# Low parts of weights by adding DMAs in place of sums on VectorE and GpSimd

## The chip, the core and the metric

The kernel runs on one core of one Trainium2 chip. The metric is device time in microseconds (us) of one execution. Engines go by their names in the profile: PE (TensorE matmuls) and PEld (its weight loads), DVE (VectorE), ACT (ScalarE), POOL (GpSimd) and SP (SyncE, which here only issues DMAs).

## What is computed

A trunk of two pre-norm residual layers on 1024 tokens of 1024 channels. Cut to its core, the reference is:

```python
for i in range(2):
    mod = silu(c) @ ada_w[i] + ada_b[i]                 # adaLN: 6 vectors of 1024
    sh_m, sc_m, g_m, sh_f, sc_f, g_f = split(mod, 6)
    h = rms_norm(x, norm_mix_g[i]) * (1 + sc_m) + sh_m
    y = conformer_conv(h) if i == 0 else multiscale_pool(h)
    x = x + (1 + g_m) * y
    h = rms_norm(x, norm_ffn_g[i]) * (1 + sc_f) + sh_f
    x = x + (1 + g_f) * ((silu(h @ w_gate[i]) * (h @ w_up[i])) @ w_down[i])   # width 2816
return rms_norm(x, final_g)
```

`conformer_conv` is a product to 2048 channels with a gated linear unit, a causal depthwise convolution of width 31 over the tokens, a layer norm with swish, and a product back to 1024 channels. `multiscale_pool` takes trailing means over 2, 4, 8 and 16 tokens and four small products. Everything is float32.

## The kernel before

**Tiling.** Channels lie on the 128 partitions, tokens along the free dimension. The tokens are two chunks of 512, A and B. A weight tile is 128 x 1024 floats (512 KB): for a product with 1024 input channels it holds eight 128 x 128 blocks.

**Split products.** PE runs in the format float32r. To keep float32 precision, both operands are split into a high part (rounded to float32r) and a low part (the remainder), and each product is three matmuls: high x high, high x low and low x high (`products`, L378). So each weight tile has a buffer of twice its size: `wt[:, 0]` is the high part and `wt[:, 1]` the low part. A tile is used in 24 matmuls of 512 columns.

**Loading a weight** (`load_weight`, L369). SP loads the raw tile into a buffer of the pool `raws` (L147, three buffers: `RAW_BUFS`, L37). ACT copies it to `wt[:, 0]`, which rounds it. Then DVE or POOL writes `wt[:, 1] = raw - wt[:, 0]`; `either` (L139) picks the engine whose planned clock is earlier. The pool `wts` has six buffers (`W_BUFS`, L36). A raw buffer is free again when both readers are done, and the buffers of a pool are used in turn.

**The adaLN vectors** use the same pool `raws`. For layer 0, `ada_columns` (L334) loads tiles of `adan` in pairs and multiplies them on PE. For layer 1 and its later vectors, `ada_task` (L296) loads tiles of `ada` one by one, and DVE forms a dot product in place on each (`ada_dot`, L292); SP issues these loads in the same queue as those of the weights. There are 32 tiles of `adan` and, after the start, 48 of `ada`.

**Order.** The order on PE is written by hand: a list of units, each with the weight tiles that it uses. `run_units` (L509) emits them in turn, and its `ahead` (L516) calls `load_weight` for tiles of later units, so that up to six are loaded or in use. Other work (convolution taps, norms, adaLN, pooling) consists of tasks that `pace` (L169) steps between units. A planner keeps a clock for each engine, with a fixed price for each kind of instruction (`PRICES`), and gives a step to DVE or POOL when that clock is not ahead of PE's. A scheduler then sets the final order of the engines other than PE.

**The convolution's taps** (`Taps`, L579) are 31 steps for each of 16 tiles of 128 x 512. DVE adds a tap in one instruction, into `ca`. On POOL, ACT first forms the product `pr`, and POOL adds it to `pa`. DVE joins the two at the end.

**Course.** The first stage computes the first adaLN vectors and, with eight tiles loaded for it alone, half of the first product for chunk A. Then come the rest of the first product for A and B with the taps of A behind it, the layer norm and output product of A, the feed-forward part of layer 0 for A with the taps of B behind it, the output product of B, the feed-forward part of layer 0 for B with the adaLN vectors of layer 1, and layer 1. A feed-forward unit uses two tiles (gate and up); after each group of three units comes one with three tiles (down).

In the rows below, nearly all instructions of DVE, ACT and POOL have the line L95, and PE's L117, since a helper issues them; L372 is the load of a weight, L127 and L134 are other loads.

Of the kernel before, what the change touches and what calls it, by code (L numbers as in the profile page):

```python
# [9 lines left out]
F32 = mybir.dt.float32  # L10
F32R = mybir.dt.float32r
I32 = mybir.dt.int32
AF = mybir.ActivationFunctionType
ALU = mybir.AluOpType
MUL, ADD, SUB = ALU.mult, ALU.add, ALU.subtract

P = 128
D = 1024
# [82 lines left out]
def trunk(ctx, tc, xT, c, vec, ada, adan, w1, w2, wgu, wdn, wpl, out):  # L101
    nc = tc.nc
    ctx.enter_context(tc.manual_schedule(engines={mybir.EngineType.PE}))
    clock = {"PE": 0.0, "V": 0.0, "G": 0.0, "S": 0.0}
    V_ = Engine(nc.vector, "V", clock, PRICES["V"], lambda i: order(i))
    G_ = Engine(nc.gpsimd, "G", clock, PRICES["G"], lambda i: order(i))
    S_ = Engine(nc.scalar, "S", clock, PRICES["S"], lambda i: order(i))
# [11 lines left out]
    def order(ins):  # L119

        if behind[0] and last_mm[0] is not None:
            tc.add_manual_dep(ins.ins, last_mm[0], edge, reason="behind the products")
        return ins
# [15 lines left out]
    def either(n):  # L139

        now = clock["PE"]
        v, g = (max(clock[e], now) + engines[e].price("tensor_tensor", n) for e in "VG")
        return V_ if v <= g else G_
# [9 lines left out]
    def nm(s):  # L153
        uid[0] += 1
        return f"{s}_{uid[0]}"
# [13 lines left out]
    def pace(ahead=AHEAD):  # L169

        for t in [t for t in tasks if t.urgent or getattr(t, "free", False)]:
            while step(t, "V"):
                pass
        moved = True
        while moved and tasks:
            moved = False
            for e in "VG":
                if clock[e] < clock["PE"] + ahead:
                    moved = any(step(t, e) for t in list(tasks)) or moved
# [186 lines left out]
        return mod[:, b : b + 1]  # L366


    def load_weight(src, n=D, load=nc.sync.dma_start):  # L369
        raw = raws.tile([P, D], F32, tag="raw", name=nm("raw"))[:, :n]  # L370
        dst = raw if len(src.shape) == 2 else raw.rearrange("p (a b) -> p a b", a=src.shape[1])
        load(dst, src)  # L372
        wt = wts.tile([P, 2, D], F32R, tag="w", name=nm("w"))
        S_.copy(wt[:, 0, :n], raw)
        either(n).tensor_tensor(wt[:, 1, :n], raw, wt[:, 0, :n].bitcast(F32), op=SUB)
        return wt

# [131 lines left out]
    def run_units(cap, early):  # L509

        queue = [w for ws, _ in units for w in ws]
        loaded = list(early)
        del queue[: len(early)]
        used = [0]

        def ahead(free):  # L516
            while queue and len(loaded) + used[0] - free < cap:
                loaded.append(load_weight(queue.pop(0)))
                if len(loaded) > 1:
                    break  # L520

        for ws, emit in units:
            def take():
                ahead(0)
                used[0] += 1
                return loaded.pop(0)
            emit(take)
            used[0] -= len(ws)
            ahead(0)
            pace()  # L530
# [379 lines left out]
    for k in range(KT + 1):  # L910
        if k < KT:
            w = wts.tile([P, 2, D], F32, tag="w", name=nm("adaw"))
            load_next(w, ada_m[0, k][:, 0:2, :])
            ada_dot(w[:, 1], 0, 1, k)
            tc.add_manual_dep(V_.last.ins, t_last if k else rstd_last, edge, reason="behind the first norm")
        if k > 0:
            dot = V_.last.ins.name
            V_.scalar_tensor_tensor(h_a[k - 1][1], t, mod[:, k - 1 : k], h_a[k - 1][0].bitcast(F32), op0=ADD, op1=SUB)
            if k < KT:
                tc.add_manual_dep(V_.last.ins, dot, edge, reason="the scalar engine's part takes that long")  # L920
            for q in range(2 * FIRST):
                products(fb[q], wt, q, h_a[k - 1], k == 1, k == KT)
        if k < KT:
            ada_dot(w[:, 0], 0, 0, k)
            V_.tensor_scalar(scale_m[:, k : k + 1], mod[:, KT + k : KT + k + 1], scale_b[:, k : k + 1], V("norm_mix_g", k), op0=ADD, op1=MUL)
            V_.tensor_tensor(mod[:, k : k + 1], mod[:, k : k + 1], V("ada_b", k), op=ADD)
            t = temp(A.n)
            V_.scalar_tensor_tensor(t, x[0][k], scale_m[:, k : k + 1], rstd_a, op0=MUL, op1=MUL)
            t_last = V_.last.ins.name
            S_.activation(h_a[k][0], t, AF.Identity, bias=mod[:, k : k + 1])  # L930
            wt = load_weight(w1k[k], 2 * FIRST * P, load_next)
    for e in clock:
        clock[e] = max(clock.values())
    early = [load_weight(w1[FIRST, i], load=load_next) for i in range(2)]
    for k in range(KT):
        load_next(x[1][k], xT[:, k, B.t0 : B.t0 + B.n])
# [154 lines left out]
```

## Time and profile before

| What | Value |
|---|---|
| Median of 3 runs | 1996.76 us (1985.09 to 1997.44) |
| Time of the profiled execution | 1995.5 us |
| Its span, first to last instruction | 1993.7 us |
| Mean granted TensorE clock | 0.957 of full speed |
| DMA packets and bytes | 71800, 223.91 MB, mean 112 GB/s |

How to read the profile: busy time is the time in which an engine executes; an engine's idle time matters only where PE, or another engine on the chain, waits for it. Matmuls are pipelined, so the mean of one matmul (some 390 ns) is longer than the distance between two. A group row has count, busy time, mean, and the idle time ahead of it with what ended it. DMA issues show the issuing engine's time; the transfer itself is in "us to landing". In the table by stage each row is a stretch of the span. The prediction shows the rows that it uses.

### The profile page before, as it was taken

How to read it: one execution, taken by the hardware profiler on the slowest of the kernel's cores; microseconds unless marked ns; L12 is line 12 of the kernel's file. 1: busy time of each engine (PE TensorE's matmuls, PEld its weight loads, DVE VectorE, ACT ScalarE, POOL GpSimd, SP SyncE). 2: the span in 40 equal slices, each digit the busy share in tenths (PEclk: the TensorE clock that was granted, in tenths of full speed). 3: DMA queues.
4: the chain of work that ended last, by engine and by line, in shares of the span. 5: the costliest groups of instructions: out<-in, count | busy, mean ns of one | idle time of the engine just before them, and what ended most of it. 6: DMA issues, size and time to landing. Idle time of an engine off the chain costs nothing.

```text
span 1993.7 us, 21104 instructions
## 1 busy us (share of the span) xinstructions
PE 1831.9 (92%) x8016; PEld 1483.9 (74%) x8016; DVE 1195.3 (60%) x1554; ACT 711.9 (36%) x979; POOL 772.2 (39%) x533
## 2 busy tenths in 40 slices
PE   6999639788989998689999999999999999999997
PEld 4776417677767886567888888888888888888886
DVE  8889863789984346678846333585563346333334
ACT  3555543555633223223323222342332232222223
POOL 4678942699933213225512111262122221211111
PEclk9999858899999999799999999999999999999998
DMA  8534422122222236374322222323222223222221
GB/s 271 207 107 141 144 84 96 53 85 86 84 85 85 95 124 225 108 251 159 104 98 96 95 95 95 106 81 109 96 96 95 96 95 127 95 96 95 96 94 43
DMA packets 71800, 223.91 MB, mean 112 GB/s; under 512 B 7057, under 2 KB 17425, under 8 KB 71698
## 3 DMA queue, kind: packets, MB, share of 16 engines
q1 hardware_dynamic: 70544, 221.51, 33.2%
q8 instruction: 63, 1.03, 0.2%
q10 hardware_dynamic: 1154, 1.05, 0.2%
q14 instruction: 39, 0.32, 0.1%
HBM read 218.34 MB, written 4.19 MB: 112 GB/s over the span
## 4 chain that ended last, share of the span: by engine, by line
PE 63%; DVE 12%; POOL 10%; issue 6%; DMA 6%; ACT 2%; SPq 0%; DVEq 0%; POOLq 0%; ACTq 0%
PE dn L117 22%; PE gate L117 18%; PE up L117 17%; POOL pa L95 7%; PE y L117 3%; DMA adaw<-in_ada_dram 3%; DVE adaw L95 2%; POOL w L95 2%; DVE acc L95 1%; DVE w L95 1%; DMA raw<-in_w_dram 1%; DVE col L95 1%; DVE t L95 1%; DVE ca L95 1%; DVE x L95 1%
## 5 line engine op out<-in xcount | busy, mean ns | idle before, releaser
L95 POOL TENSOR_TENSOR w<-raw,w 128x1024 fp32r<-128x1024 f32 x148 | 371.0, 2508 | 971.1 <-ACT w L95 952.3
L95 ACT CAST w<-raw 128x1024 fp32r<-128x1024 f32 x312 | 321.2, 1046 | 635.5 <-issue 384.7
L117 PE MATMUL dn<-ghi,w 128*128 128x512 f32 (+1 forms) x1456 | 454.4, 391 | 20.9 <-ACT ghi L95 19.8
L117 PE MATMUL gate<-hhi,w 128*128 128x512 f32 x1408 | 456.1, 393 | 10.4 <-ACT w L95 5.8
L117 PE MATMUL up<-hhi,w 128*128 128x512 f32 x1408 | 454.3, 392 | 0.0
L117 PEld LDWEIGHTS dn<-ghi,w 128*128 128x128 f32 x1456 | 275.8, 192 | 82.3 <-ACT ghi L95 22.3
L117 PEld LDWEIGHTS gate<-hhi,w 128*128 128x128 f32 x1408 | 266.3, 189 | 69.1 <-ACT w L95 6.7
L95 DVE TENSOR_TENSOR t<-t,up 128x512 f32<-128x512 f32 x88 | 60.2, 684 | 412.3 <-PE up L117 405.3
L117 PEld LDWEIGHTS up<-hhi,w 128*128 128x128 f32 x1408 | 266.0, 189 | 55.4
L95 POOL TENSOR_TENSOR pa<-pa,pr 128x512 f32<-128x512 f32 x201 | 286.2, 1445 | 39.0 <-ACT pr L95 34.6
L117 PE MATMUL dn<-glo,w 128*128 128x512 f32 (+1 forms) x728 | 286.0, 393 | 14.4 <-DVE glo L95 9.4
L95 DVE TENSOR_TENSOR w<-raw,w 128x1024 fp32r<-128x1024 f32 x164 | 249.3, 1521 | 56.8 <-ACT w L95 52.8
L95 DVE SCALAR_TENSOR_TENSOR x<-dn,gains,x 128x512 f32<-128x512 f32 (+1 forms) x264 | 190.8, 730 | 154.2 <-PE dn L117 154.0
L117 PE MATMUL gate<-hlo,w 128*128 128x512 f32 x704 | 276.1, 392 | 1.1 <-DVE hlo L95 1.1
L117 PE MATMUL up<-hlo,w 128*128 128x512 f32 x704 | 275.3, 391 | 0.0
L117 PEld LDWEIGHTS dn<-glo,w 128*128 128x128 f32 x728 | 139.4, 191 | 46.1 <-DVE glo L95 11.2
L95 DVE SCALAR_TENSOR_TENSOR ca<-u,vecs,ca 128x512 f32<-128x512 f32 x247 | 172.7, 746 | 0.9
L95 ACT ACTIVATE pr<-u,vecs 128x512 f32<-128x512 f32 x201 | 140.3, 720 | 81.1 <-POOL pa L95 70.6
L117 PEld LDWEIGHTS gate<-hlo,w 128*128 128x128 f32 x704 | 133.4, 189 | 29.4 <-DVE hlo L95 1.6
L117 PEld LDWEIGHTS up<-hlo,w 128*128 128x128 f32 x704 | 133.0, 189 | 27.4
L95 ACT ACTIVATE t<-gate 128x512 f32<-128x512 f32 x88 | 52.5, 597 | 252.9 <-PE gate L117 233.0
L95 DVE SCALAR_TENSOR_TENSOR adaw<-adaw,cact 128x1024 f32<-128x1024 f32 x64 | 86.8, 1358 | 36.0 <-DMA adaw<-in_ada_dram 35.4
(115 smaller groups left out, 1628.1 us busy)
## 6 DMA issues: line engine op xcount, KB each, us to landing
raw<-in_wgu_dram SPq DMA_DIRECT2D x176, 512.0 KB, 3.3
raw<-in_wdn_dram SPq DMA_DIRECT2D x88, 512.0 KB, 3.4
adaw<-in_ada_dram SPq DMA_DIRECT2D x48, 512.0 KB, 4.3
raw<-in_w_dram SPq DMA_DIRECT2D x44, 512.0 KB, 3.5
adan<-in_adan_dram SPq DMA_DIRECT2D x32, 512.0 KB, 4.4
adaw<-in_ada_dram SPq DMA_DIRECT2D x8, 1024.0 KB, 6.7
x<-in_xT_dram SPq DMA_DIRECT2D x16, 256.0 KB, 5.0
raw<-in_wpl_dram SPq DMA_DIRECT2D x4, 512.0 KB, 3.3
```

Of the source, the lines that this page charges most:

```text
L95: self.last = self.order(getattr(self.eng, name)(out, *args, **kw))
L117: last_mm[0] = nc.tensor.matmul(out, lhsT, rhs, start=start, stop=stop).ins.name
```

## The change

`load_weight` gets a parameter `summed`, which `run_units` sets for every tile that it loads; the eight tiles of the first stage and the two that are loaded early call it without. With it, ACT writes a second copy of the raw tile, negated, to `wt[:, 1]`, which rounds to the negated high part. Then a DMA, issued on POOL's queue, adds the raw tile to it in SBUF: raw - high, the low part. The planner's clock of POOL is advanced by 1.0 for it. The raw buffer is free when the DMA has read it. The scratch space for descriptors of such DMAs grows from 256 to 1024 bytes per partition.

```diff
-    def load_weight(src, n=D, load=nc.sync.dma_start):
+    def load_weight(src, n=D, load=nc.sync.dma_start, summed=False):
         raw = raws.tile([P, D], F32, tag="raw", name=nm("raw"))[:, :n]
         dst = raw if len(src.shape) == 2 else raw.rearrange("p (a b) -> p a b", a=src.shape[1])
         load(dst, src)
         wt = wts.tile([P, 2, D], F32R, tag="w", name=nm("w"))
         S_.copy(wt[:, 0, :n], raw)
+        if summed:
+            S_.activation(wt[:, 1, :n], raw, AF.Copy, scale=-1.0)
+            order(nc.gpsimd.dma_start(wt[:, 1, :n].bitcast(F32), raw, accum_op=ADD))
+            clock["G"] = max(clock["G"], clock["PE"]) + 1.0
+            return wt
         either(n).tensor_tensor(wt[:, 1, :n], raw, wt[:, 0, :n].bitcast(F32), op=SUB)
         return wt
...
-                loaded.append(load_weight(queue.pop(0)))
+                loaded.append(load_weight(queue.pop(0), summed=True))
...
-    nc = _bacc.Bacc("TRN2", target_bir_lowering=False, num_devices=1, dynamic_dma_scratch_size=256)
+    nc = _bacc.Bacc("TRN2", target_bir_lowering=False, num_devices=1, dynamic_dma_scratch_size=1024)
```

## The prediction, made before the changed kernel ran

> **What bounds the kernel now.** I read, in this order, the page's busy shares, its chain of work, the busy time by stage, the chain inside the stages that are not full, and the queue of loads on SP.
>
> ```profile
> span 1993.7 us, 21104 instructions
> ...
> PE 1831.9 (92%) x8016; PEld 1483.9 (74%) x8016; DVE 1195.3 (60%) x1554; ACT 711.9 (36%) x979; POOL 772.2 (39%) x533
> ```
> ```profile
> PE 63%; DVE 12%; POOL 10%; issue 6%; DMA 6%; ACT 2%; SPq 0%; DVEq 0%; POOLq 0%; ACTq 0%
> PE dn L117 22%; PE gate L117 18%; PE up L117 17%; POOL pa L95 7%; PE y L117 3%; DMA adaw<-in_ada_dram 3%; DVE adaw L95 2%; POOL w L95 2%; DVE acc L95 1%; DVE w L95 1%; DMA raw<-in_w_dram 1%; DVE col L95 1%; DVE t L95 1%; DVE ca L95 1%; DVE x L95 1%
> ```
>
> PE carries the chain, but not everywhere. The table by stage says where it does not (stretch and its length; busy time and count on PE, weight loads, DVE, ACT, POOL; granted clock; DMA share; GB/s):
>
> ```profile
> 62.00:235.00 173.00, 162.55 (x740) 123.03 (x738) 151.35 (x191) 98.69 (x141) 137.95 (x111) 0.98 0.42 144
> 235.00:305.00 70.00, 21.38 (x75) 9.16 (x75) 45.75 (x77) 31.96 (x51) 38.35 (x30) 0.55 0.30 102
> ...
> 350.00:620.00 270.00, 237.86 (x982) 191.59 (x981) 231.14 (x303) 145.98 (x206) 206.38 (x136) 0.92 0.24 78
> 620.00:715.00 95.00, 95.00 (x419) 78.30 (x418) 32.98 (x37) 24.54 (x30) 19.28 (x8) 1.00 0.28 95
> 715.00:980.00 265.00, 226.23 (x957) 182.86 (x956) 191.08 (x249) 79.73 (x107) 100.54 (x87) 0.92 0.51 170
> 980.00:1960.00 980.00, 980.00 (x4341) 808.73 (x4340) 446.76 (x540) 280.04 (x359) 221.93 (x105) 1.00 0.29 96
> ```
>
> Of the 1994 us, 620 to 715 and 980 to 1960 are PE alone: it is full at clock 1.00, and DVE, ACT and POOL are busy for under half of the time. Nothing taken from them shortens these 1075 us. The rest is in three places: the taps of the first half (to 305), the taps of the second half (350 to 620, DVE 86% and POOL 76% busy), and the adaLN stage (715 to 980), where DMA is at 0.51.
>
> In the full stages one weight tile lasts PE 5.44 us (24 products), which is the rate at which new ones are needed:
>
> ```profile
> 1150.56 5.48 PE gate L117 x24
> 1156.03 5.44 PE up L117 x24
> ```
>
> **What the change does, part by part.** In the built kernels' instruction order, 302 of the 312 weight tiles lose their sum on DVE or POOL and get one ACT instruction (the negated high part) and one DMA issued on POOL's queue that adds the raw tile. The eight tiles of the first stage and two loaded early keep the sum. PE's products are the same. SP's order of loads hardly changes. The planner also moves 26 taps from POOL to DVE (191 steps left on POOL, where there were 217).
>
> The prices of the parts, from the instructions on the tile raw (min/median/max ns) and from the page's DMA parts:
>
> ```profile
> L95 ACT CAST w<-raw x312: 1028/1046/1057, 14.9 to 1943.6; 128x1024 fp32r<-128x1024 f32 x156
> L372 SPq DMA_DIRECT2D raw<-in_wgu_dram x176: 327/328/408, 302.7 to 1912.6; - x176
> L95 DVE TENSOR_TENSOR w<-raw,w x164: 1206/1226/2752, 62.5 to 1939.3; 128x1024 fp32r<-128x1024 f32 x164
> L95 POOL TENSOR_TENSOR w<-raw,w x148: 2338/2393/3963, 16.0 to 1944.7; 128x1024 fp32r<-128x1024 f32 x148
> ```
> ```profile
> q1 hardware_dynamic: 70544, 221.51, 33.2%
> ...
> raw<-in_wgu_dram SPq DMA_DIRECT2D x176, 512.0 KB, 3.3
> ...
> adaw<-in_ada_dram SPq DMA_DIRECT2D x8, 1024.0 KB, 6.7
> ```
>
> *ACT.* 302 x 1.05 = 317 us more, less 26 x 0.7 for taps that leave: about 1010 us, half of the span. In the fullest stretch, 350 to 620, it has 146 of 270 busy and gets some 39 x 1.05 = 41: no bound. Price zero in itself; what covers it is ACT's idle time, and without that each negation would delay the casts and taps queued behind it by 1.05 us.
>
> *The issue on POOL.* No row shows it. Below: an issue on SP, 0.33 us. Above: the sum that it replaces, 2.39 us. I take 1.0, between them and nearer to the issue, as POOL reads no tile for it. The issue waits for the negation, 1.05 us later than the sum did, with POOL's taps queued behind it.
>
> *The adding transfer.* No row shows one either. It reads two tiles of 512 KB and writes one. Below: a load of 512 KB, 3.3 us. Above: a load of 1024 KB, 6.7 us. For the value between: 221.51 MB took 33.2% of 1993.7 us on 16 engines, so 512 KB cost 1.57 us of all engines, and the second read adds that to a landing of 3.4: 5.0 us. In a sentence of its own: the Trainium skill (DMA: Bandwidth & Descriptors, section Anatomy of one DMA) gives a POOL-issued DMA about 2.0 us plus bytes / 436 GB/s, 3.2 us for 512 KB as an estimate, which would make the sum below about 2010 us; no run here shows it yet.
>
> *How long a raw tile is held.* This is the step that decides, because there are three raw buffers for weights and adaLN tiles together, used in turn, with SP's loads in order. Before: load 3.4, cast 1.05, sum 1.23 or 2.39, together 6.2 on average. After: load 3.4, cast and negation 2.1, issue 1.0, transfer 5.0: 11.5. Each weight holds its buffer 5.3 us longer (with the bounds above, 2.9 to 8.4). The sum's place goes to a wait of SP: behind it stand all later loads, and behind those ACT's casts (in order, with the taps' products behind them) and PE.
>
> Where PE is full, three buffers give a tile every 11.5 / 3 = 3.8 us against 5.44, and up to six weight tiles are in hand: hidden, price zero. It would cost if the hold went above 16.3 us, or if the DMA engines became the limit (a rival below).
>
> In the first half, two of the three buffers are held by adaLN tiles that wait for PE, and the weights pass through one. SP's queue (start, length, issues) and the chain there:
>
> ```profile
> 206.94 0.81 SPq L127 DMA_DIRECT2D adan<-in_adan_dram  x2
> 212.39 5.92 SPq L372 DMA_DIRECT2D raw<-in_w_dram  x2
> 219.05 0.80 SPq L127 DMA_DIRECT2D adan<-in_adan_dram  x2
> 224.94 5.90 SPq L372 DMA_DIRECT2D raw<-in_w_dram  x2
> ```
> ```profile
> 210.00 2.38 POOL w L95
> 212.39 3.23 DMA raw<-in_w_dram
> 215.65 1.06 ACT w L95
> 216.73 1.24 DVE w L95
> 217.98 3.38 DMA raw<-in_w_dram
> ```
>
> A load follows straight on the sum that frees its buffer; a pair takes 224.94 - 212.39 = 12.6 us, as much as PE needs for two tiles and its adaLN products. Four such pairs get 2 x 5.3 longer each: 42 us. Most of it is covered, because PE is through with these products early and then waits for the taps:
>
> ```profile
> PEld mean L117 <- DVE acc L95: 37.3, 1, 37.3
> ```
>
> That wait covers 37 us, so 5 are left; for the earlier weights of this half, whose delay starts taps late, I add 10 (an estimate: two weights' 5.3): +15 us.
>
> In the adaLN stage 48 tiles run through the same buffers between weights, and the chain goes from one landing to the dot product that frees the buffer and on to the next load:
>
> ```profile
> 738.60 5.41 DMA adaw<-in_ada_dram
> 744.04 1.24 DVE adaw L95 x2
> 745.30 4.33 DMA adaw<-in_ada_dram
> ```
>
> By the built order of SP, weights stand at nine places among the 48. Each pushes the in-order chain by 5.3: 48 us. I take two thirds, 32 us (an estimate): PE is busy for 226 of the 265 us, so part of the push falls where it has tiles in hand. DMA share is highest here, too, so nothing makes it cheaper.
>
> What the sums' leaving gives, stretch 62 to 305 and 350 to 620 (instructions on the tile w, same columns):
>
> ```profile
> 62.00:305.00 243.00, 146.25 (x621) 116.67 (x619) 25.09 (x17) 26.13 (x25) 21.91 (x9) 0.86 0.38 132
> ...
> 350.00:620.00 270.00, 231.82 (x948) 185.88 (x947) 45.96 (x27) 40.12 (x39) 28.88 (x12) 0.92 0.24 78
> ```
>
> In the second taps stage DVE loses 46 us and POOL 29; POOL gets 39 issues of 1.0 and loses about half of the 26 taps (13 x 1.4 = 18, which cost DVE 13 x 0.75 = 10). POOL, whose taps are on the chain, is left with 39 - 29 - 18 = 8 us less: -8, and DVE's 36 us are mostly not on the path; I take -10. In the first taps stage any gain only shortens that cover and is not counted. At the end (after 1960) no weight is left: zero.
>
> Sum, against the profiled execution's 1995.5 us (span 1993.7 and 1.8 around it; it stands 1.3 below the median of 1996.76): 1995.5 + 15 + 32 - 10 = 2032.5, so **2033 us**. With all lower prices (2.9 us of hold, 0.33 an issue) the terms are 0, 9 x 2.9 x 2/3 = 17 and -25, 1988; with all upper ones (8.4 us, 2.39 an issue, the adaLN push in full) 67 - 37 + 17 = 47, 76 and +30, 2149.
>
> **Rivals.**
>
> *It gets faster: the hold is covered everywhere.* For it: six tiles in hand last PE 33 us, DVE and POOL are nearly full in the taps, and 44 sums of DVE (71 us) and 21 of POOL (51 us) go there against 65 issues: 122 - 65 = 57 us of engine time, half of it on each: -28, so 1967 us. Against it: the chain above steps from sum to load. It decides if a weight is held no more than about 2 us longer, a transfer that lands in 2 us.
>
> *No change.* The lower prices above: gain and loss cancel, about 1995 us.
>
> *The DMA engines become the bound.* Loads take 1.57 us of each 5.44. If the add takes three such shares, 4.7, a tile costs 6.3 and every full stage is 0.84 us per tile longer: 4760 products / 24 = 198 tiles, 167 us, and with the 37 above 2200 us; four shares would give 2510. It decides from 3.9 us of service per add. Against it: two reads are two shares, 3.1 us, together 86% of 5.44. The Trainium skill (Collectives: The Full Stack, section The bandwidth ceiling) says that an adding DMA runs at half of a copy's rate because it reads two sources, not because of the sum; by that rule this rival falls, and no row here shows it.
>
> *The issue costs POOL as much as the sum did.* At 2.4 us, POOL has 65 x 1.4 = 91 us more in the taps than I counted; with half of it on the path, 2079 us. For it: POOL is the slow engine. Against it: in the full stages it would not matter.
>
> **How the numbers follow.** Forecast (slower by holds, 2018 to 2149): 0.47. Issue as dear as the sum: 0.12. DMA engines as the bound: 0.13. No change: 0.11. Faster: 0.17. About 1% is what a measurement of this kernel can tell from none; faster by over 1% is 0.17, within 1% 0.11, slower 0.72. The range runs from 1968, at the rival that ends faster, to 2200, at the DMA rival's mildest case; half of each lies outside, about 0.15 to 0.2. The likeliest case's own range is 2018 to 2149.
>
> **What the changed profile would show.** Right: the full stages unchanged at 5.44 us per tile; SP's loads waiting for the adding DMA, not for DVE or POOL; landings near 5 us; the adaLN stage some 30 us longer; PE's wait for the taps of the first half shorter, as its products end later; fewer PE gaps in 350 to 620. Wrong: landings under 3 us or over 8; a DMA share near 1 and tiles of over 5.5 us in the full stages; POOL idle or busy for over 2 us at each issue; a taps stage that is longer than before.

## The result and the profile after

The changed kernel takes 2012.47 us (median of 4 runs, 2009.98 to 2017.11); the kernel before, measured beside it, 1993.28 us (median of 4, 1985.09 to 1997.44). The ratio is 1.0101, interval 1.0079 to 1.0123: slower by 1%, 19 us. The prediction was 2033 us, slower, with 1968 to 2200 as its range; the range of its likeliest case was 2018 to 2149, and the measured time lies below that. The profiled span goes from 1993.7 to 2008.2 us, 14.5 longer.

The page of the changed kernel, busy shares and the chain that ended last:

```profile
span 2008.2 us, 21898 instructions
...
PE 1841.0 (92%) x8016; PEld 1485.6 (74%) x8016; DVE 912.8 (45%) x1422; ACT 971.9 (48%) x1255; POOL 620.5 (31%) x665
```
```profile
PE 72%; DMA 11%; DVE 7%; ACT 4%; issue 4%; POOL 2%; SPq 0%; DVEq 0%; POOLq 0%; ACTq 0%
```

DVE lost 283 us of work and POOL 152, with the issues of its 302 DMAs (269 us) counted in; ACT, which had room, took 260 more. On the chain DVE and POOL together fell from 22% to 9%, PE rose from 63% to 72%, and DMA from 6% to 11%. So the change does what it says, and the time comes back through the DMAs. What they cost, from the DMA part of the same kernel (queue: packets, MB, share of 16 engines; then KB each and median us to landing):

```profile
q0 software_dynamic: 43488, 158.35, 43.4%
q1 hardware_dynamic: 70544, 221.51, 32.6%
...
w<-raw POOLq DMA_DIRECT2D x302, 512.0 KB, 5.9
raw<-in_wgu_dram SPq DMA_DIRECT2D x176, 512.0 KB, 5.0
```

An add (one adding DMA) lands 5.9 us after its issue began, and a load that runs beside adds takes 5.0 where it took 3.3. An add takes 0.434 x 2008.2 / 302 = 2.89 us of all 16 engines; a load, 512 KB of the 221.51 MB, 1.55. The instructions on the tile raw (min/median/max ns):

```profile
L95 ACT ACTIVATE w<-raw x302: 1046/1054/1064, 71.0 to 1965.5; 128x1024 fp32r<-128x1024 f32 x151
L377 POOL DMA_DIRECT2D w<-raw x302: 832/869/2009, 72.6 to 1966.9; - x151
```

Where the 14.5 us arise is read from two products that stand at the same place in PE's order in both kernels: the output product (y<-vhi; it starts with chunk A behind the first taps and ends with chunk B) and the pooling product (y<-mxhi), whose first matmul follows the adaLN stage. Rows of the tile y, "first start to last start", before and then after:

```profile
L117 PE MATMUL y<-vhi,w x256: 388/389/774, 305.0 to 782.0; 128*128 128x512 f32 x128
...
L117 PE MATMUL y<-mxhi,w x64: 389/389/390, 1022.9 to 1436.2; 128*128 128x512 f32 x64
```
```profile
L117 PE MATMUL y<-vhi,w x256: 388/389/796, 318.0 to 779.0; 128*128 128x512 f32 x128
...
L117 PE MATMUL y<-mxhi,w x64: 389/389/389, 1036.5 to 1449.8; 128*128 128x512 f32 x64
```

That cuts the span into four parts. The first half (to 305.0) is 13.0 us longer, the part with the second taps and output product B (305.0 to 782.0) 16.0 shorter, the adaLN stage (782.0 to 1022.9) 16.6 longer; the rest, up to the last gate product, takes 930.7 us in both. With 0.9 behind that: 13.0 - 16.0 + 16.6 + 0.9 = 14.5. The full stages did not move; a stretch of 50 us in one, with all engines (PE, weight loads, DVE, ACT, POOL, clock, DMA share, GB/s), and the chain in another:

```profile
1500.00:1550.00 50.00, 50.00 (x221) 41.17 (x220) 10.04 (x14) 21.05 (x24) 7.82 (x9) 1.00 0.83 191
```
```profile
1213.37 5.44 PE gate L117 x24
1218.81 5.44 PE up L117 x24
```

PE is busy all the time, 5.44 us a tile, though DMA stands at 0.83 there: 2.89 + 1.55 = 4.44 of each 5.44 us is 0.82.

**The first half after.** SP's queue (start, length, issues), and the chain beside it:

```profile
195.45 11.29 SPq L372 DMA_DIRECT2D raw<-in_w_dram  x4
...
221.15 0.80 SPq L372 DMA_DIRECT2D raw<-in_w_dram  x2
222.04 9.75 SPq L127 DMA_DIRECT2D adan<-in_adan_dram  x2
237.81 0.80 SPq L372 DMA_DIRECT2D raw<-in_w_dram  x2
```
```profile
195.45 3.33 DMA raw<-in_w_dram
...
199.81 1.05 ACT w L95
...
201.26 5.10 DMA w<-raw
...
206.41 5.83 DMA raw<-in_w_dram
...
213.28 1.06 ACT w L95
...
214.74 6.36 DMA w<-raw
...
221.15 3.24 DMA raw<-in_w_dram
```

A load starts some 0.05 us after an add has landed, where it used to follow a sum. Raw tiles are held for 10.9 us (195.45 to 206.36), 14.7 (206.41 to 221.1) and 16.2 (the second load of the pair at 221.15 to 237.76). But the two loads of a pair are issued within 0.80 us (they took 5.92 before): they lie in two buffers side by side, and a pair takes 237.81 - 221.15 = 16.7 us against 12.6.

### The profile page after: what moved, and what is told of

Its sections match the earlier page's. It is cut to its first block, busy times and chain, and to the rows that moved or that the text cites. A ratio compares the mean times of both kernels' runs of the same rounds, so it can differ in the third digit from the quotient of the medians.

```text
span 2008.2 us, 21898 instructions
## 1 busy us (share of the span) xinstructions
PE 1841.0 (92%) x8016; PEld 1485.6 (74%) x8016; DVE 912.8 (45%) x1422; ACT 971.9 (48%) x1255; POOL 620.5 (31%) x665
## 3 DMA queue, kind: packets, MB, share of 16 engines
q0 software_dynamic: 43488, 158.35, 43.4%
q1 hardware_dynamic: 70544, 221.51, 32.6%
## 4 chain that ended last, share of the span: by engine, by line
PE 72%; DMA 11%; DVE 7%; ACT 4%; issue 4%; POOL 2%; SPq 0%; DVEq 0%; POOLq 0%; ACTq 0%
PE dn L117 22%; PE gate L117 21%; PE up L117 20%; DMA w<-raw 4%; PE y L117 3%; DMA adaw<-in_ada_dram 3%; PE first L117 2%; ACT w L95 2%; POOL pa L95 2%; DVE ca L95 2%; DVE acc L95 1%; DVE adaw L95 1%; DMA raw<-in_w_dram 1%; DMA raw<-in_wdn_dram 1%; PE g L117 1%
## 5 line engine op out<-in xcount | busy, mean ns | idle before, releaser
L95 ACT CAST w<-raw 128x1024 fp32r<-128x1024 f32 x312 | 325.3, 1043 | 745.5 <-PE dn L117 244.7
L377 POOL DMA_DIRECT2D w<-raw x302 | 269.1, 893 | 1161.1 <-ACT w L95 1068.8
L117 PE MATMUL dn<-ghi,w 128*128 128x512 f32 (+1 forms) x1456 | 454.7, 391 | 34.7 <-ACT ghi L95 14.8
L95 ACT ACTIVATE w<-raw 128x1024 fp32r<-128x1024 f32 x302 | 318.4, 1054 | 0.0
L95 POOL TENSOR_TENSOR pa<-pa,pr 128x512 f32<-128x512 f32 x175 | 247.5, 1552 | 27.3 <-ACT pr L95 24.4
L95 DVE SCALAR_TENSOR_TENSOR ca<-u,vecs,ca 128x512 f32<-128x512 f32 x273 | 187.9, 747 | 0.9
L95 DVE TENSOR_TENSOR glo<-t,ghi 128x512 fp32r<-128x512 f32 x75 | 55.5, 740 | 237.7 <-ACT ghi L95 237.7
L95 ACT ACTIVATE pr<-u,vecs 128x512 f32<-128x512 f32 x175 | 118.8, 716 | 35.5 <-POOL pa L95 26.2
L95 DVE SCALAR_TENSOR_TENSOR adaw<-adaw,cact 128x1024 f32<-128x1024 f32 x64 | 79.3, 1245 | 55.8 <-DMA adaw<-in_ada_dram 55.6
```

Source lines behind the costliest of these rows:

```text
L95: self.last = self.order(getattr(self.eng, name)(out, *args, **kw))
L117: last_mm[0] = nc.tensor.matmul(out, lhsT, rhs, start=start, stop=stop).ins.name
L377: order(nc.gpsimd.dma_start(wt[:, 1, :n].bitcast(F32), raw, accum_op=ADD))
```

## The experiments

**The theories.** *Holding (H):* the loss comes from raw tiles that are held longer by the negation, the issue and the transfer, while SP's in-order loads wait for one of three buffers. Its rivals: *traffic*, the bytes of the adds that slow the other loads; and *POOL's issue*, with POOL's taps queued behind a DMA that waits for its operand. In the code, `at[0]` counts the weight tiles that `run_units` loads: 0 to 25 belong to the first half and output product A, 87 to 114 to output product B and the adaLN stage, together 54.

All parts of the span, read as above (us; "ratio" is the time against the kernel before, measured beside it on the same chip, with its interval):

| Kernel | to output product A | A to end of B | adaLN stage | rest | Median | Ratio |
|---|---|---|---|---|---|---|
| before | 305.0 | 477.0 | 240.9 | 930.7 | 1993.28 | 1 |
| after | 318.0 | 461.0 | 257.5 | 930.7 | 2012.47 | 1.0101 (1.0079 to 1.0123) |
| e1_rest_only | 302.0 | 454.4 | 237.4 | 930.7 | 1966.85 | 0.9887 (0.9859 to 0.9915) |
| e2_first_only | 318.5 | 472.3 | 241.0 | 930.7 | 2004.18 | 1.0066 (1.0050 to 1.0083) |
| e3_ada_only | 298.5 | 487.9 | 252.8 | 930.8 | 2016.17 | 1.0135 (1.0107 to 1.0163) |
| e4_hold_add | 317.6 | 468.8 | 259.7 | 930.8 | 2024.16 | 1.0168 (1.0142 to 1.0193) |
| e5_traffic_add | 340.3 | 470.8 | 255.9 | 930.7 | 2041.55 | 1.0270 (1.0252 to 1.0288) |
| e6_after_w5r5 | 289.9 | 455.1 | 230.2 | 930.7 | 1951.56 | 0.9821 (0.9805 to 0.9837) |
| e7_after_w5r3 | 326.7 | 470.8 | 270.5 | 953.2 | 2048.98 | 1.0322 (1.0283 to 1.0361) |
| e8_before_w5r5 | 292.5 | 477.5 | 222.0 | 930.7 | 1962.24 | 0.9863 (0.9845 to 0.9881) |
| e9_before_w5r3 | 296.4 | 474.8 | 243.2 | 930.7 | 1988.03 | 0.9995 (0.9978 to 1.0011) |
| e10_traffic_act | 310.8 | 477.8 | 244.4 | 930.7 | 2000.76 | 1.0070 (1.0047 to 1.0093) |
| e11_issue_add | 321.9 | 468.1 | 244.9 | 930.7 | 2007.81 | 1.0110 (1.0085 to 1.0134) |
| e12_not_ada_w5r5 | 293.0 | 443.5 | 221.5 | 930.7 | 1931.18 | 0.9726 (0.9702 to 0.9751) |

The parts come from one profiled execution each. How far they can be trusted shows where kernels are alike: the first half of e1 and e3 is that of before, and the three read 298.5 to 305.0. Differences of under some 7 us in one cell prove nothing. The profiled execution is not always near the median either: that of e7 took 2063.4 us, 14 above its median, and that of e3 2012.6, 4 below.

### Adding DMAs in some stages only (e1 to e3)

The same edit with three conditions:

```diff
-                loaded.append(load_weight(queue.pop(0), summed=True))
+                at[0] += 1
+                loaded.append(load_weight(queue.pop(0), summed=not (at[0] < 26 or 87 <= at[0] < 115)))   # e1
+                loaded.append(load_weight(queue.pop(0), summed=at[0] < 26))                              # e2
+                loaded.append(load_weight(queue.pop(0), summed=87 <= at[0] < 115))                       # e3
```

> Adding DMAs only for weights outside the first half and the adaLN stage (the 54 weights there keep the sums on DVE and POOL). Theory H (a raw tile is held longer, and that costs only where adaLN tiles share the three raw buffers; elsewhere the change gains or is free): the loss of the two places goes and the gain in the second taps stage stays, some 13 us below the kernel before, about 1980 us. Rival T (adding DMAs slow the other transfers wherever they run): the loss is spread over all stages, and the time lies between the two kernels, about 2000. Rival N (the gain in the second taps stage came from the other order of the first half): no gain, about 1993.

> Adding DMAs only for the 26 weights of the first half (first products for A and B, output product of A). Theory H: the output product of A starts 13 us later than before, as in the changed kernel (318 for 305), and little gives it back: about 2006 us. Rival P (the first half lost time through the planner's shift of taps to DVE, not through the loads): the loads' pairs take 12.6 us as before.

> Adding DMAs only for 28 weights in and beside the adaLN stage. Theory H: the stretch from the output product of B to the pooling product is 14 to 17 us longer than before, about 2009 us. Rival T: that stage's loss came from adding DMAs of its neighbourhood as well, so less than half of it, under 2001.

Measured: the rest alone is 23.8 us faster than before (1990.65 beside it), which is 13 more than holding expected. The first half alone is 13.5 slower, as expected. The 28 tiles of output product B and the adaLN stage alone are 25.5 slower, 7 more than expected, though the adaLN stage itself grew by 11.9, less than the 14 to 17 forecast. The sum, -23.8 + 13.5 + 25.5 = +15, is near the +19 of the whole change. So the whole loss comes from 54 of the 302 tiles, and the other 248 gain 24 us, nearly all of it (22.6) in the part with the second taps. The planner's shift of taps to DVE does not explain e2: its pairs of loads start 16.4 us apart (221.78 to 238.18), not 12.6. One more thing shows in the part with the second taps: e3 is 10.9 slower there, and has adds there only in output product B's tiles. PE's waits in the changed kernel, from 318 to 779 us (us in total, times, longest):

```profile
PE y L117 <- ACT w L95: 6.5, 1, 6.5
PE y L117 <- DMA w<-raw: 4.7, 1, 4.7
```

PE stands for 11.2 us at output product B, for ACT's work on its tiles and for the add. e3 has the same two waits (5.7 and 4.6 us); e1, with sums there, has neither.

### More raw buffers, with and without the change (e6 to e9)

This kernel's tiles leave no room in SBUF for a fourth raw buffer beside six weight buffers, so one weight buffer (8 KB per partition) is given up for two raw ones (4 KB each), and the kernels with five weight buffers and three raw ones serve as controls:

```diff
-W_BUFS = 6
-RAW_BUFS = 3
+W_BUFS = 5
+RAW_BUFS = 5    # e6 on the changed kernel, e8 on the kernel before; e7 and e9: 3
```

> The changed kernel with five weight buffers instead of six and five raw buffers instead of three (memory does not hold four beside six). Theory H: two more raw buffers take the wait out of the loads, so the adaLN stage and the first half lose less than in the next run, which has three: 15 to 40 us below it. Rival T: no difference to it, within 5 us.

> The changed kernel with five weight buffers and three raw buffers, the comparison for the run before: one tile less in hand, no other change. Both theories: the changed kernel's time or some us more, 2010 to 2030.

> The kernel before with five weight buffers and five raw buffers. If the raw buffers bound the adaLN stage before the change already, as its chain of loads and dot products says, it gains too, but less than the changed kernel does (shorter hold): 5 to 20 us below 1993. If only the adding DMAs made raw buffers scarce: no change or some us more for the missing weight buffer.

> The kernel before with five weight buffers and three raw buffers: with the three runs that have five weight buffers it makes a square of sums or adding DMAs by three or five raw buffers. Theory H: with three raw buffers the adding DMAs cost far more than with five, where they gained (1951.6 against 1962.2): this run is 20 us or more below 2049, so 2029 or less. Rival T (traffic alone): the difference between sums and adding DMAs is the same with three as with five buffers, so this run is at 2049 or above.

Measured: with three raw buffers the adds cost 2048.98 - 1988.03 = 61 us; with five they gain 1962.24 - 1951.56 = 11 us. In the source, nothing but the number of raw buffers differs between these two comparisons: the adds, their bytes and their issues on POOL are the same. The sizes were not foreseen: e7 was expected at 2010 to 2030, e6 15 to 40 us below it (it is 97 below), and e8 at 5 to 20 below 1993 (it is 31 below). The tile y of e7 and then of e6:

```profile
L117 PE MATMUL y<-vhi,w x256: 387/389/795, 326.7 to 797.5; 128*128 128x512 f32 x128
...
L117 PE MATMUL y<-mxhi,w x64: 389/389/390, 1068.0 to 1489.9; 128*128 128x512 f32 x64
```
```profile
L117 PE MATMUL y<-vhi,w x256: 387/389/792, 289.9 to 745.0; 128*128 128x512 f32 x128
...
L117 PE MATMUL y<-mxhi,w x64: 388/389/390, 975.2 to 1388.5; 128*128 128x512 f32 x64
```

By the table, the adds cost the first half 326.7 - 296.4 = 30 us with three buffers and -3 with five; the adaLN stage 27 and 8. The products of the first half show it directly: the last one starts 46 us later with adds than with sums when there are three raw buffers (271.4 against 225.3), and 3.5 later when there are five (230.1 against 226.6). That is what holding says. It does not say which part of the hold costs most: a load that traffic slows also holds its buffer longer, and more buffers hide that as well. The full stages show the other side: those of e7 are 22.5 us longer, with these waits of PE behind 1068 us:

```profile
PE dn L117 <- DMA w<-raw: 14.3, 11, 2.4
```

So the cover of the full stages, too, is made of buffers: with six weight and three raw buffers there was no such wait, with five and three there are eleven, with five and five again none. And e8 says that the kernel before was short of raw buffers as well: 1.4% faster without any add.

### The hold, the traffic and the issue, one at a time (e4, e5, e10, e11)

All four keep the sums on DVE and POOL and add something to the 54 tiles. e4 lets POOL issue a DMA of 512 bytes that writes from the finished low part into a column of the raw tile, so the raw buffer is free only when it has landed (the column is not used any more). e11 issues the same small DMA to a place of its own, so that only the issue is left. e5 copies both parts of the tile to memory on POOL's queue, and e10 copies the high part twice on ACT's queue, right behind the cast: traffic without a hold.

```diff
         either(n).tensor_tensor(wt[:, 1, :n], raw, wt[:, 0, :n].bitcast(F32), op=SUB)
+            order(nc.gpsimd.dma_start(raw[:, 0:1], wt[:, 1, 0:1].bitcast(F32)))                 # e4
+            order(nc.gpsimd.dma_start(apart[:, i : i + 1], wt[:, 1, 0:1].bitcast(F32)))         # e11
+            for part in range(2): order(nc.gpsimd.dma_start(spill[j], wt[:, part].bitcast(F32)))  # e5
+            for part in range(2): order(nc.scalar.dma_start(spill[j], wt[:, 0].bitcast(F32)))     # e10, ahead of the sum
```

> The sums stay on DVE and POOL for all weights; for the 54 of the first half and the adaLN stage a DMA on POOL's queue writes one column of the finished low part over the first column of the raw tile, which nobody reads any more. It moves 512 bytes, and the raw buffer is free only when it has landed. Theory H: a hold some 3 us longer, half of the change's 5.3, so a third to two thirds of the two losses together (13 + 17): 2003 to 2013 us. Rival T (traffic of the adding DMAs): no traffic, so no change beyond POOL's issues, 1993 to 1998.

> The sums stay on DVE and POOL; for the 54 weights of the first half and the adaLN stage two DMAs on POOL's queue copy the high and the low part to unused device memory: two tiles of traffic beside the loads, about what an adding DMA moves, and no raw buffer is held for it. Theory H: nothing but POOL's issues, 1990 to 2000 us. Rival T: most of the two losses (13 + 17), 2010 to 2025.

> The traffic test again without POOL: sums as before, and for the 54 weights of the first half and the adaLN stage two DMAs on ACT's queue copy the high part to unused device memory, right behind the cast. No raw buffer is held for it and no engine waits on another for it. Theory H: 1990 to 1998 us, with the taps of the first half ending near 267 as before, and the loss of 51 us in the run with copies on POOL's queue was POOL's. Rival T: the adaLN stage is again 10 to 15 us longer, and the time 2003 to 2025.

> POOL's issue by itself: as the run whose small DMA held the raw tile (2024 us), but the 512 bytes go to a column of their own, so that POOL issues and waits for the sum as there, and no raw tile is held. If the hold made that run slow, the adaLN stage falls back to some 241 us from its 260; what remains of the 33 us, in the first half's taps, is POOL's issue and its wait: 1998 to 2012 us. If the issue on POOL made it slow everywhere: 2018 to 2026.

In the adaLN stage the hold stands out: the hold and the issue cost 18.8 us (259.7 against 240.9), the issue alone 4.0, traffic alone 3.5 (each of these two within what a cell can tell). The difference of e4 and e11, the hold, is 14.8; the change costs 16.6 there, with a hold of another length. In medians, each against the kernel before beside it, e4 loses 33.5 us and e11 18.6, so the hold costs 15. The loss of e4 is larger than was expected of it (2003 to 2013 us): the issue comes on top of the hold, and the sum stays in front of both. The wait that e4 puts into SP's queue, and that the kernel before has not:

```profile
SPq L127 <- DMA raw<-w: 116.1, 18, 19.7
```

In the first half they are not clear. e11 is as late there as the change itself, without any hold: 321.9. Its small DMAs wait on POOL until DVE has made a sum, and POOL's taps stand behind them. The tile apart, with the idle time of POOL ahead of its issues (us in total, times):

```profile
L380 POOL DMA_DIRECT2D apart<-w x54: 534/552/773, 74.0 to 934.2; - x54
...
  DVE w L95: 31.4, 13
```

The changed kernel has a wait like it: in its first half POOL stands for 50 us ahead of the adds (62 to 305 us: 28.8 for ACT's work on the weight, 13.1 for other work of ACT, 8.5 put down to a load). But the loss does not come about in the same way. In e11 the last product of the first half starts 11.9 us later than before (241.6 against 229.7), and PE's wait for the taps behind it gets longer (PE's waits in e11, 62 to 305 us):

```profile
PE mean L117 <- DVE acc L95: 50.1, 1, 50.1
```

Before, that wait was 36.4 us. In the changed kernel the last product starts 32.2 us later and the wait falls to 21.0: there the products are late, not the taps. e6 against e8 agrees: with the change's issues and bytes, and 40 us of such waits, but five buffers, the first half loses nothing. So e11 shows that an issue on POOL that waits for DVE can cost as much as the hold, not that the change pays it.

e5 does not decide. It came out at +54 us (1987.86 before), above what either theory gave, but two more instructions per tile on POOL, each waiting, stand ahead of taps and sums, and its 35 us in the first half can't be told from e11's. e10 is the cleaner one. Its two copies read as many bytes per tile as an add, and one lands like an add:

```profile
spill<-w ACTq DMA_DIRECT2D x108, 512.0 KB, 5.6
```

It costs 0.7% (0.47 to 0.93) in all, 11.5 us by the medians; of that 3.5 in the adaLN stage and 5.8 in the first half. Its time of 2000.76 lies between what holding (1990 to 1998) and traffic (2003 to 2025) expected. So traffic may have a part, smaller than the hold's. The parts do not add up (15 for the hold, 19 for an issue, 11.5 for traffic, against the 39 that e2 and e3 lose together), and with kept sums they need not.

### A version that beats both (e12)

e12 takes five weight and five raw buffers, and the adds everywhere but in the 28 tiles of output product B and the adaLN stage, where e6 still lost 8.2 us against e8.

```diff
+W_BUFS = 5
+RAW_BUFS = 5
...
+                loaded.append(load_weight(queue.pop(0), summed=not (87 <= at[0] < 115)))
```

> Five weight and five raw buffers, adding DMAs everywhere but for the 28 weights of the adaLN stage. With all weights by adding DMAs that stage took 230 us, with sums 222; if the parts add up, 8 us less than 1951.6: about 1943 us. If the stage's loss came from its neighbours' traffic, 1950 or more.

Measured: 1931.18 us (1930.64 to 1935.5), ratio 0.9726 (0.9702 to 0.9751): 2.7% faster than the kernel before, 81 us faster than the change as made, and 12 better than the 1943 expected. Its page:

```profile
span 1929.1 us, 21843 instructions
...
PE 1809.2 (94%) x8016; PEld 1472.0 (76%) x8016; DVE 959.3 (50%) x1428; ACT 949.4 (49%) x1227; POOL 652.8 (34%) x659
```

Against e6, the adaLN stage gives 8.7 us and the part before it 11.6 (output product B has its sums back); against e8, the taps stage gives 34.0 and nothing is lost elsewhere.

## Why the prediction was right, step by step

The direction and the mechanism were right. The size was forecast about twice too large: 37 us against the 19 of the medians. The 0 for the full stages was right, the first half came out close by luck, and the largest term, that of the adaLN stage, was twice too big.

**Direction and mechanism: right, and shown.** The sums' place was taken by SP's wait for the adding DMA. SP's waits before (us in total, times, longest), and then in the changed kernel:

```profile
SPq L372 <- DVE w L95: 824.6, 148, 27.1
SPq L372 <- POOL w L95: 566.2, 104, 18.8
...
SPq L127 <- DVE w L95: 50.5, 10, 25.0
```
```profile
SPq L372 <- DMA w<-raw: 1427.4, 273, 26.1
...
SPq L127 <- DMA w<-raw: 125.0, 22, 15.6
```

Most of the 1427 us is free: 853 of them stand behind 1037 us, where PE is full. What costs lies in the stages with adaLN tiles (e1 to e3). e6 to e9 show that it is the buffers.

**Full stages, 0: right.** 930.7 us in both kernels. By the medians a hold is 5.0 for the load, 2.1 for cast and negation, 0.4 until POOL issues (from the end of the negation at 213.28 + 1.06 to 214.74) and 5.9 for the add: 13.4 us, under the 16.3 that the prediction named as the limit, and the DMA engines are at 0.83. In e7, with one weight buffer fewer, PE begins to wait. The rival with the DMA engines as the bound needed 3.9 us of service per add; it was 2.89. The Trainium skill (Collectives: The Full Stack, section The bandwidth ceiling) says of a collective's reduce step that it runs at about half of a copy's rate because its add needs two source reads; the trace comes near it, with 2.89 / 1.55 = 1.86 times the service of a load from memory for each add.

**The parts of the hold.** Issue and transfer of the add: 5.9 us, of which the issue is 0.87 (taken: 1.0 + 5.0 = 6.0). A load beside adds: 5.0 (3.4). The pause of 0.4 ahead of the issue was not counted. Hence 13.4 us by the medians, and 10.9 to 16.2 in the places read above, where 11.5 was taken. The load was the step overlooked: its duration came from a trace without adds. The sum by the Trainium skill (DMA: Bandwidth & Descriptors, section Anatomy of one DMA), an estimate of 3.2 us for the landing, is not what was measured: 5.9 us in the median, in a kernel whose DMA engines are 76% busy with these two queues (43.4 + 32.6). The measurement decides.

**First half, +15: measured +13.0, by luck: two wrong sizes cancel.** The delay was taken as four pairs, each longer by two holds, 42 us, with 10 more for earlier tiles. A pair grew by 4.1 us only, since its two loads now run side by side; the last product of the stage still starts 32.2 us later (261.9 against 229.7), by earlier tiles as well. The cover was taken as all of PE's wait for the taps, 37 us:

```profile
PEld mean L117 <- DVE acc L95: 24.3, 2, 21.4
```

21.4 of it are left, so it covered 15.9 of the 32.2. The likely reason, which no run isolates, is that some taps can only be made once the last product is there, however early the others are: a wait is a cover only as far as the work that ends it does not itself follow on what is delayed.

**adaLN stage, +32: measured +16.6. This is the term that was mis-sized.** The prediction charged nine places with 5.3 us each and took two thirds. On the chain from 779 to 1037 us the adds stand only four times:

```profile
841.75 4.55 DMA w<-raw
...
883.90 7.13 DMA w<-raw
...
906.44 4.94 DMA w<-raw
...
934.65 7.32 DMA w<-raw
```

SP's queue there, after and then before: a run of eight adaLN loads with the weight loads ahead of it, and the first six loads in a row behind the adaLN tiles:

```profile
875.26 1.59 SPq L372 DMA_DIRECT2D raw<-in_wdn_dram  x2
878.69 19.02 SPq L127 DMA_DIRECT2D adaw<-in_ada_dram  x8
...
929.27 26.57 SPq L372 DMA_DIRECT2D raw<-in_wgu_dram  x6
```
```profile
866.72 2.87 SPq L372 DMA_DIRECT2D raw<-in_wdn_dram  x2
871.23 15.57 SPq L127 DMA_DIRECT2D adaw<-in_ada_dram  x8
...
914.56 12.40 SPq L372 DMA_DIRECT2D raw<-in_wgu_dram  x6
```

Eight loads behind a pair of weights take 3.4 us longer, not 5.3 per tile: while a weight holds one buffer, the others go on. The last adaLN issues end at 911.77 us, 8.4 later than before (903.39), though output product B was through 3.0 us earlier (779.0 against 782.0): 11.4 of the 16.6 us come up to there, where the term had 32. The other 5.2 come behind, when the tiles in hand are filled again: the six loads take 26.57 us instead of 12.40, and the fourth add, 934.65, lies there. That place had no term of its own.

**Second taps, -10: measured -16.0.** e1, with the sums kept in output product B's tiles, shows -22.6 for the sums that leave; PE's 11.2 us of waiting at output product B give part of it back. The prediction had no cost for those tiles. The taps themselves end much earlier (the last mean of the second half starts at 544.8 us where it started at 574.5), but PE can only use what it stood idle for.

The sum was 1995.5 + 15 + 32 - 10 = 2033; with the measured parts, 1995.5 + 13.0 + 16.6 - 16.0 + 0.9 = 2010.0, the profiled execution's time. The prediction's lower and upper sums, 1988 and 2149, hold -25 and +30 for the second taps, where its own figures give 39 x 0.33 - 47 = -34 and 39 x 2.39 - 47 = +46; neither changes the forecast. The rival "faster because the hold is covered everywhere" comes true as soon as there are buffers to cover it (e6 against e8), with 11 us instead of its 28. The rival of the dear issue falls: 0.87 us where it needed 2.4. Two of the signs that the prediction named against itself were badly chosen. POOL does stand over 2 us at an issue (1161.1 us ahead of 302 issues in the changed kernel), most of it (some 745 us) in the full stages, where it costs nothing; and the taps of the first half do end later, by the forecast's own +15.

**What stays open.** How much of the 8.2 us that e6 still loses in the adaLN stage is traffic and how much hold was not separated, nor whether e10's 11.5 us come from slower loads or from ACT's own issues (0.44 us each in the median). POOL's taps also became slower in the changed kernel (median 1562 ns against 1297). The traces tell where, not why: in the second taps the median is 1593 to 1597 ns in the kernels that run adds there (after, e1, e6, e7, e12) and 1297 to 1305 in the others. In the first half it is 1317 in the changed kernel and 1522 in e6, and 1287 in e5, whose full copies POOL issues there.

## What to carry to other kernels

When work moves from an engine to a DMA, count how long each buffer is held, with all loads priced at the rate that they have beside the new traffic, and look first at the stages where few buffers are shared by two kinds of tiles in one in-order queue. A full PE hides a longer hold only while the hold divided by the raw buffers stays under a tile's time (13.4 / 3 against 5.44 us here), and even that did not suffice with one weight buffer fewer. The same edit lost 61 us with three raw buffers and gained 11 with five. Before such an edit is dropped or kept as a whole, try it per stage: here 248 tiles gained 24 us and 54 lost 39.

## What the runs showed of the hardware

- An adding DMA within SBUF of 512 KB: 0.87 us of issue on POOL, landing 5.9 us after the start of the issue (medians), 2.89 us of 16 engines' service.
- POOL's taps (128 x 512) took 1.6 us in the median in the second taps with such adds, 1.3 without.
- Loads of 512 KB from memory beside such adds land in 5.0 us where they took 3.3; the adaLN tiles, 4.4 against 4.3, hardly changed.
- A DMA of 512 bytes on POOL's queue costs 0.55 us of issue and lands in 1.7 us (e4) or 3.1 (e11); to hold a 512 KB buffer with it cost 15 us over 54 tiles.
